# Two-layer attention encoder in float32: where layer B's memory projection runs, how memory turns and grid bias transfers are ordered

## The chip, the cores and the metric

One Trainium2 chip, one of its cores. The metric is device time of one launch in microseconds (us), smaller being better. The core has TensorE (PE, matrix products), VectorE (DVE), ScalarE (ACT), GpSimd (POOL) and SyncE (SP); in this kernel SP issues every transfer, so all transfers stand in one queue in the order in which SP reaches them.

## The reference

The kernel computes two encoder layers over 1024 tokens of width 1024, all in float32. Each layer normalises its input, projects it, runs 12 token heads and 4 memory heads side by side, projects their outputs together, and adds a SwiGLU block of width 2816. Layer A's token heads see a window of 128 tokens either side, with a position bias and a sink logit; layer B's see a neighbourhood on a 16 x 64 grid, with a bias by row and column distance. The memory heads attend to 256 memory rows, normalised with a gain of each layer's own and projected to keys and values:

```python
for i in range(DEPTH):
    h = rms_norm(x, norm_mix_pre[i])
    m = rms_norm(mem, norm_mem[i])
    mkv = jnp.einsum('bmd,de->bme', m, w_mem_kv[i])      # 256 key and 256 value columns
    ...
    mem_out = memory_attn(qm, mk, mv)
    mixed = jnp.einsum('bse,ed->bsd', jnp.concatenate([tok, mem_out], axis=-1), w_out[i])
    x = x + rms_norm(mixed, norm_mix_post[i])
    ...
```

So layer B's memory keys and values depend on the memory alone, and can be made at any time before layer B's memory heads.

## The kernel before, in words

**Arithmetic.** Every product runs as three matmuls (`mm3`, lines 90 to 93) on values split in two: a high part made by ACT (a copy that rounds) and a low part, the remainder, made by DVE or POOL (`split_ps` line 95 from PSUM, `split_raw` line 113 for weights). A weight unit is 128 x 1024 floats: one 512 KB transfer into `wr` (2 buffers), ACT's copy on line 115, the remainder on line 116 (by POOL in the opening, by DVE during the attention: `low`, lines 111 and 609), into a ring of 3 buffers.

**Order.** PE's order is the program's own (the `manual_schedule` blocks of lines 585 and 776). The other engines' instructions and SP's transfers are put in order by a scheduler at build time, by priority (program order, moved by `high_priority` offsets) and by when it estimates them to be ready; an engine then runs its instructions strictly in that order. `keep_in_program_order` ties one instruction behind the one traced just before it on the same engine. `LATER` and `LKS` (60 and 40) lower the priority of the splits of queries and of the opening's keys.

**Opening (lines 585 to 599).** PE turns the 8 normalised token tiles and projects layer A's values from them (`first_values`). Then a loop runs over c = 0, 1. For each c it normalises the two memory tiles with layer c's gain (`memory_rows`), projects the first half of layer A's key unit c (8 steps of 3 matmuls, each 512 columns wide), turns the memory in 4 blocks of 4 transposes (`memory`), projects the second half of the key unit, and runs `memory_kv(c)`: two units by `proj_T` and a pair of units by `proj_N`, 96 matmuls of 256 columns. Layer A's results (c = 0) stay on the chip save one half of the keys; layer B's (c = 1) go to DRAM (`mem_scr`, lines 573 and 574). The projections use two PSUM banks (`psG`), the turns two others (`psT`). Each key half is split into four operand planes by a chain of 4 ACT and 4 DVE instructions on 64 partitions (`k_split`, lines 226 to 229), after which its bank is free. After c = 0 `bias_tables` writes layer A's bias vectors to DRAM (`vec_d`).

**Attention.** `heads` (line 301) walks 8 groups of 16 units in `ORDER` = 0, 6, 1, 7, 2, 3, 4, 5: groups 0 to 5 are pairs of token heads, 6 and 7 pairs of memory heads. A unit is 128 queries of one head. PE does its scores (lines 254 and 255), DVE adds the bias and takes the maximum (269), ACT the exponential (272), POOL the normalisation (274); three units later PE turns the result (282), and two units after that multiplies it with the values (292). Between those, PE is fed with *filler*: the projection that the next group needs, at one step of 3 matmuls per unit, since a group's filler is one query item of 16 steps in layer A (`q_item`). The last group of layer A has no filler:

```python
groups = [(units_by[c], needs[n] if n is not None else []) for c, n in zip(order, order[1:] + [None])]
```

**Queries.** In layer A `q_tiles` (line 203) writes a projected half (512 queries) with one ACT and one DVE instruction on 128 partitions, into `q` and a single-buffered `ql`, and then three SBUF-to-SBUF transfers (`move`, line 201) bring the pieces to their partitions. In layer B it writes them in place, with two ACT and two DVE instructions on 64 partitions (lines 215 to 218) and no transfer. Units 0 to 7 of a group read the first half, units 8 to 15 the second.

**Grid bias.** Layer B's bias table is built in DRAM by 64 small transfers (`grid_tables`, line 367; all issued on line 372): 8 fills from the mask, 32 of `rpb` rows in runs of 32 bytes, 24 from `rpb_d` to `bias_d`. They are traced in five batches of 8, 16, 16, 16 and 8, one when each of pairs 0 to 4 begins, behind that group's bias loads (`bias_tiles`, line 702).

**After the attention** the 8 units of the output projection go through the same ring (lines 853 to 862).

Of the kernel before, what the change touches and what calls it, by code (L numbers as in the profile page):

```python
# [18 lines left out]
P = 128  # L19
D = 1024  # L20
# [46 lines left out]
def build(nc, tc, ctx, x_in, mem_in, wts, t5, onehot, sinks, rpb, maskb, gains, out):  # L67
# [54 lines left out]
    def load_unit(u, where=None, n=3):  # L122
        return split_raw(u, load_raw(u), where or ring, n)

    def proj_T(unit, src, n, dst):

        h, lo = unit
        for c0 in range(0, n, HALF):
# [22 lines left out]
    def run(steps):  # L151
        for _ in steps:
            pass
# [46 lines left out]
    def move(o, i):  # L200
        dma.dma_start(out=o.bitcast(F32), in_=i.bitcast(F32))

    def q_tiles(p, ps, w):

        t = p.tile([P, 2, HALF], F32R, name="q", tag="q", bufs=4)
        if windowed:
            lo = at2.tile([P, HALF], F32R, name="ql", bufs=1)
            nc.scalar.activation(t[:, 0, :w], ps, AF.Copy, scale=SCALE)
            nc.vector.scalar_tensor_tensor(lo[:, :w], ps, SCALE, t[:, 0, :w].bitcast(F32),
                                           ALU.mult, ALU.subtract)  # L210
            move(t[HIGH, 1, :w], t[HIGH, 0, :w])
# [155 lines left out]
    def grid_tables():  # L367

        def go(out, in_):
            return lambda: dma.dma_start(out=out, in_=in_)

        def fill(k, lo, hi, c, m):

            n = (hi - lo) * ROWS
            src = maskb[c * ROWS:(c + 1) * ROWS, m * P:m * P + n]
            return go(rpb_d[k][:, :, lo:hi].rearrange("h r d k -> r h (d k)"),
                      src[:, None].broadcast_to([ROWS, 12, n]))

        fills = [fill(0, lo, min(lo + 8, 31), 0, 0) for lo in range(0, 31, 8)]
        fills += [fill(1, *a) for a in ((0, 7, 7, 1), (7, 15, 0, 0), (15, 23, 0, 0), (23, 31, 0, 3))]
        steps = [fills]
        for k, ds in enumerate((slice(0, 31), slice(7, 23))):
            steps.append([])
            for r in range(ROWS):
                rs = min(max(r - 4, 0), ROWS - 8)
                steps[-1].append(go(rpb_d[k][:, r, ds, rs:rs + 8], rpb[:, ds, 15 - r + rs:23 - r + rs]))
        for k in range(2):
            steps.append([])  # L390
            src = rpb_d[k][0:1, 0:1, 7:8, 0:1]
            for c in range(8):
# [15 lines left out]

    act_d = [dpool.tile([3, FH, P, HALF], F32, name=f"act_d{k}") for k in range(DEPTH)]
    both_d = [dpool.tile([4, FH, P, D], F32, name=f"both_d{k}") for k in range(DEPTH)]  # L410
    mem_scr = dpool.tile([DEPTH, 4, P, 256], F32, name="mem_scr")

    def load_x(t, src, i, grid):
# [77 lines left out]
            return proj_T(unit, src_h, S, put)  # L491
        return (lambda: load_unit(u)), steps, 16 * 1024

    def q_item(u, keep):
        def steps(unit):
            def put(c0, w, ps):
                with tc.high_priority(offset=-LATER):
                    keep(c0 // HALF, q_tiles(a1, ps, w))
            return proj_T(unit, src_h, S, put)
        return (lambda: load_unit(u)), steps, 16 * 1024  # L500

# [14 lines left out]
    def now(item):  # L516
        run(item[1](item[0]()))
# [37 lines left out]
        g = gain(npool, 2 * DEPTH + layer, f"g{layer}")  # L555
        return [norm_rows(npool, raw_tile(mem_in, i), g, 2) for i in range(2)]

    def memory(rows):
        mT = [[a1.tile([P, 2, HALF], F32R, name="mT", tag="q", bufs=4).rearrange(
            "p a (b t) -> p (a b) t", t=MEM) for _ in range(2)] for _ in range(2)]  # L560
        for i in range(2):

            def put(b, pt, i=i):
                split_ps(pt, *(mT[k][b][:, :, i * P:(i + 1) * P] for k in range(2)))

            turn(pp["psT"], "pst", rows[i], put)
        return lambda kc, cs: tuple(mT[k][kc // 4][:, kc % 4, cs] for k in range(2))

    def memory_kv(layer, src):
        def keep(k, ps):  # L570
            if layer or k == 1:
                t = npool.tile([P, 256], F32, name="mraw", bufs=2)
# [7 lines left out]
        u0 = U_MEM + 4 * layer  # L580
        for c in range(2):
# [19 lines left out]
    apart[0] = False  # L601
    grid_todo = grid_tables()

    x_cur = x_in
    for layer in range(DEPTH):
# [61 lines left out]
        def keep_q(c, qts=qts):  # L667
            return lambda half, t: qts.__setitem__((c, half), t)
# [23 lines left out]
        if windowed:  # L692
# [13 lines left out]
            def group(p, order=order):  # L706
                c = p // 3
                pr = pair_of(p, lambda: kts[c], lambda b: vts[b], 2 * c)

                def bias(hh, j):  # L710
                    b = biases[p, hh]
                    if j == 0:
                        return b[:, 1:3]
                    return b[:, 0:2] if j == NT - 1 else b

                def units():
                    if p < 5:
                        bias_tiles(p + 1)
                    for step in grid_todo.pop(0) if grid_todo else []:
                        step()  # L720
                    if p == order[2]:
                        mem_back(1)
                    return units_of(pr, bias, PAIRS_A[p])

                return units, [q_item(U_A + p, keep_q(p))]

            bias_tiles(0)
            um = U_A + 8
        else:
# [6 lines left out]
                    biases[p, hh] = b  # L736

            def kv_items(p):
                its = [k_item(U_B + 6 + p, lambda t: kts.__setitem__(p, t)), q_item(U_B + p, keep_q(p))]
# [29 lines left out]
        for m in range(2):  # L769
            pr = pair_of(6 + m, lambda m=m: mks[m], lambda b: mvs[b], 2 * m)  # L770
            units_by[6 + m] = lambda pr=pr: units_of(pr, None, None)
            needs[6 + m] = [q_item(um + m, keep_q(6 + m))]
        for it in needs[order[0]]:
            now(it)
        groups = [(units_by[c], needs[n] if n is not None else []) for c, n in zip(order, order[1:] + [None])]
        with tc.manual_schedule(engines=PE_ONLY):
            heads(at2, groups)
        low[0] = nc.vector
# [511 lines left out]
```

## Time and profile before

| | us |
|---|---|
| median of 3 runs | 2288.87 (2288.6 to 2290.02) |
| the profiled execution | 2287.94 |
| its span, first to last instruction | 2286.2 |
| PE busy in it | 2152.5 (94%) |
| mean granted TensorE clock | 0.981 of 2.4 GHz |

Times in the rows further down are in us from the span's start. Rows of the timeline are: start, length, engine, line, operation, output<-input, count, and in brackets how long the engine stood idle before and what released it. A matmul's length overlaps its successor's, so how fast PE goes is read from the distance of starts.

### The profile page before, as it was taken

The numbers are of one execution on the slowest core, as the hardware profiler recorded it, in microseconds if no ns is written. First come the engines' busy times: TensorE is split into PE (matmuls) and PEld (weight loads), VectorE is DVE, ScalarE is ACT, GpSimd is POOL, SyncE is SP. The second block draws the span as 40 slices with busy tenths as digits, with TensorE's granted clock in tenths as the row PEclk, the third lists the DMA queues.
The fourth block names the chain that finished last, engine by engine and source line by source line (L and its number), as shares of the span: only waits on it lengthen the run. The fifth ranks groups of instructions, "written<-read, shape, count | busy, mean of one in ns | idle before, by whom it ended". The sixth has DMA issues, their size and how long they took to land. (4 is left out here: it accounts for less than half of the span.)

```text
span 2286.2 us, 31339 instructions
## 1 busy us (share of the span) xinstructions
PE 2152.5 (94%) x10538; PEld 1783.6 (78%) x10538; DVE 1503.4 (66%) x2621; ACT 1062.8 (46%) x2158; POOL 735.5 (32%) x814
## 2 busy tenths in 40 slices
PE   7789987989999999999899999989899999999986
PEld 6678775868888888787788898868688888888865
DVE  5358775578677775556657765765887777755556
ACT  5458885453323332444447765764432333324333
POOL 3336663242333331011115433433334333311012
PEclk9899998999999999999999999999999999999998
DMA  6343344314545453866442322432255555436665
GB/s 218 81 112 89 91 135 105 114 56 159 197 162 182 167 184 108 297 193 211 156 130 70 98 70 77 133 104 104 74 180 184 175 172 180 154 130 223 192 208 168
DMA packets 152600, 333.88 MB, mean 146 GB/s; under 512 B 24791, under 2 KB 47191, under 8 KB 152440
## 3 DMA queue, kind: packets, MB, share of 16 engines
q1 hardware_dynamic: 152440, 331.88, 45.7%
q8 instruction: 84, 1.38, 0.3%
q14 instruction: 76, 0.62, 0.1%
HBM read 226.96 MB, written 92.93 MB: 140 GB/s over the span
## 5 line engine op out<-in xcount | busy, mean ns | idle before, releaser
L944 DVE TENSOR_TENSOR zt<-acc,zt 128x512 f32<-128x512 f32 x300 | 204.6, 686 | 148.8 <-PE acc L93 146.9
L1089 DVE TENSOR_TENSOR dl<-draw,dh 128x1024 fp32r<-128x1024 f32 x146 | 187.0, 1288 | 164.7 <-ACT dh L1087 164.1
L274 POOL TENSOR_TENSOR sn<-sn,st 128x384 f32<-128x384 f32 (+1 forms) x256 | 189.0, 740 | 237.5 <-DVE st L273 199.6
L1087 ACT ACTIVATE dh<-draw 128x1024 fp32r<-128x1024 f32 x146 | 153.9, 1059 | 219.8 <-PE acc L93 141.4
L92 PE MATMUL acc<-dl,dh 128*128 128x512 f32 x584 | 230.6, 395 | 15.8 <-DVE dl L1089 15.8
L93 PE MATMUL acc<-dh,dl 128*128 128x512 f32 x584 | 229.0, 392 | 0.0
L91 PE MATMUL acc<-dh 128*128 128x512 f32 x584 | 225.2, 391 | 1.9 <-ACT dh L1087 1.7
L887 ACT ACTIVATE gh<-zt 128x512 fp32r<-128x512 f32 x168 | 104.3, 628 | 167.2 <-PE acc L92 146.7
L963 POOL TENSOR_TENSOR tw<-tw 128x512 f32<-128x512 f32 x88 | 132.6, 1507 | 120.0 <-DMA tw<-in_wts 114.2
L116 DVE TENSOR_TENSOR wl<-wr,wh 128x1024 fp32r<-128x1024 f32 x88 | 112.8, 1282 | 87.7 <-ACT wh L115 86.0
L1144 POOL TENSOR_TENSOR tt<-tt,g 128x512 f32<-128x512 f32 x32 | 52.9, 1668 | 365.2 <-ACT junk L1143 365.2
L115 ACT ACTIVATE wh<-wr 128x1024 fp32r<-128x1024 f32 x100 | 105.6, 1056 | 119.7 <-DMA wr<-in_wts 85.2
L940 ACT ACTIVATE zt<-zt 128x512 f32<-128x512 f32 x84 | 53.1, 632 | 225.3 <-DVE zt L944 225.3
L963 POOL TENSOR_TENSOR zt<-zt 128x512 f32<-128x512 f32 x66 | 91.4, 1385 | 205.6 <-DVE zt L941 202.2
L92 PE MATMUL psg<-hL,wh 128*128 128x512 f32 x384 | 153.7, 400 | 0.0
L91 PE MATMUL psg<-hH,wh 128*128 128x512 f32 x384 | 153.5, 400 | 0.0
L93 PE MATMUL psg<-hH,wl 128*128 128x512 f32 x384 | 153.4, 399 | 0.0
L292 PE MATMUL psv<-PT,v 128*128 128x256 f32 x656 | 142.2, 317 | 5.2 <-DVE attn L652 3.6
L98 DVE TENSOR_TENSOR PT<-pst,PT 128x384 fp32r<-128x384 f32 (+1 forms) x256 | 126.7, 495 | 28.5 <-ACT PT L97 24.6
L92 PEld LDWEIGHTS acc<-dl,dh 128*128 128x128 f32 x584 | 110.6, 189 | 43.7 <-DVE dl L1089 21.1
L272 ACT ACTIVATE sn<-sn,st 128x385 f32<-128x385 f32 (+3 forms) x192 | 113.0, 589 | 63.7 <-DVE st L269 56.4
L889 DVE TENSOR_TENSOR gl<-zt,gh 128x512 fp32r<-128x512 f32 x168 | 130.1, 776 | 8.1 <-ACT gh L887 8.0
(218 smaller groups left out, 5965.5 us busy)
## 6 DMA issues: line engine op xcount, KB each, us to landing
wr<-in_wts SPq DMA_DIRECT2D x146, 512.0 KB
draw<-both_d SPq DMA_DIRECT2D x88, 512.0 KB
both_d<-zt SPq DMA_DIRECT2D x88, 256.0 KB
tw<-in_wts SPq DMA_DIRECT2D x44, 512.0 KB
both_d<-tw SPq DMA_DIRECT2D x44, 512.0 KB
act_d<-zt SPq DMA_DIRECT2D x66, 256.0 KB
draw<-act_d SPq DMA_DIRECT2D x66, 256.0 KB
draw<-in_wts SPq DMA_DIRECT2D x66, 256.0 KB
```

The costliest lines, as they stand in the source:

```text
L91: nc.tensor.matmul(ps, lh, rh, start=start, stop=False)
L92: nc.tensor.matmul(ps, lh, rl, start=False, stop=False)
L93: nc.tensor.matmul(ps, ll, rh, start=False, stop=stop)
L98: nc.vector.tensor_tensor(ol, ps, oh.bitcast(F32), ALU.subtract)
L272: nc.scalar.activation(sn[:, :m], sn[:, :m], AF.Exp, bias=nm, scale=-1.0, accum_out=ssum)
L274: nc.gpsimd.tensor_tensor(sf, sf, rinv.broadcast_to([P, n]), ALU.mult)
L292: nc.tensor.matmul(pv[:, j % 2], pair.v(self.lo + c)[:, pair.vh + hh], self.PT[:, c], start=c == 0, stop=c == nk - 1)
L889: nc.vector.tensor_tensor(lo, src, h.bitcast(F32), ALU.subtract)
L944: nc.vector.tensor_tensor(o, a, b, ALU.add)
L963: nc.gpsimd.tensor_tensor(o, a, b, ALU.subtract)
L1087: nc.scalar.activation(h, raw, AF.Copy)
L1089: eng.tensor_tensor(lo, raw, h.bitcast(F32), ALU.subtract)
```

## The change

1. `memory` turns a block and then takes two steps of the key projection (`pump`), four times, in place of four turns in a row and then eight steps.
2. For c = 1 the opening only turns the memory; the four turned pieces (high and low, two each, 512 KB a piece) are stored to DRAM (`mt_d`). Layer B's memory projection becomes three filler items (96 matmuls, 4 weight units) of layer A's last group, and pair 4's group begins with loading the four pieces back into a key buffer. The stores of its results to `mem_scr` stay, now from the `sn` buffers that the units use too.
3. In layer A the queries of the first and the last pair (0 and 5) are written in place, as in layer B.
4. Each of the 64 grid bias transfers is tied behind the transfer traced just before it.

`start=0` in `proj_T` is used by nothing here, and the later `apart[0] = False` has no key split of layer A's between its two places.

```diff
-    def q_tiles(p, ps, w):
+    def q_tiles(p, ps, w, apart):
...
-        if windowed:
+        if not apart:
...
         def go(out, in_):
-            return lambda: dma.dma_start(out=out, in_=in_)
+            return lambda: tc.keep_in_program_order(dma.dma_start(out=out, in_=in_))
...
+    mt_d = dpool.tile([2, 2, P, D], F32, name="mt_d")
...
-    def memory(rows):
+    def memory(rows, pump):
...
                 split_ps(pt, *(mT[k][b][:, :, i * P:(i + 1) * P] for k in range(2)))
+                for _ in range(2):
+                    next(pump)
...
-    def memory_kv(layer, src):
+    def memory_items(layer, src, raw_tile):
...
-            run(proj_T(load_unit(u0 + c), src, MEM, lambda c0, w, ps, c=c: keep(c, ps)))
-        run(proj_N([load_unit(u0 + 2), load_unit(u0 + 3)], src, 2, lambda i, ps: keep(2 + i, ps)))
+            its.append((lambda c=c: load_unit(u0 + c),
+                        lambda unit, c=c: proj_T(unit, src(), MEM, lambda c0, w, ps: keep(c, ps)), 8 * 512))
+        its.append((lambda: [load_unit(u0 + 2), load_unit(u0 + 3)],
+                    lambda units: proj_N(units, src(), 2, lambda i, ps: keep(2 + i, ps)), 16 * 512))
+        return its
...
-            src = memory(rows)
+            mT = memory(rows, gen)
+            if c:
+                for k in range(2):
+                    for b in range(2):
+                        dma.dma_start(out=mt_d[k, b], in_=mT[k][b].rearrange("p c t -> p (c t)").bitcast(F32))
             run(gen)
-            memory_kv(c, src)
+            if c == 0:
+                src = mem_src(mT)
+                for it in memory_items(0, lambda: src, lambda: npool.tile([P, 256], F32, name="mraw", bufs=2)):
+                    now(it)
+                bias_tables(npool)
             lk[0] = LK
-            if c == 0:
-                bias_tables(npool)
...
-                return units, [q_item(U_A + p, keep_q(p))]
+                return units, [q_item(U_A + p, keep_q(p), p in (order[0], order[7]))]
...
+        if windowed:
+            back = []
+
+            def reload(then=units_by[order[6]]):
+                t = a1.tile([P, 4, S], F32R, name="mTk", tag="k", bufs=2)
+                for k in range(2):
+                    for b in range(2):
+                        dma.dma_start(out=t[:, 2 * k + b].bitcast(F32), in_=mt_d[k, b])
...
+                return then()
+
+            groups[6] = reload, groups[6][1]
+            groups[7] = groups[7][0], groups[7][1] + memory_items(
+                1, lambda: mem_src(back), lambda: at2.tile([P, 3 * P + 8], F32, name="sn", bufs=TURN + SNX)[:, :256])
```

## Rows read from the trace of the kernel before

**Rows 1.** The page: busy time, share of the span and instructions of each engine.

```profile
PE 2152.5 (94%) x10538; PEld 1783.6 (78%) x10538; DVE 1503.4 (66%) x2621; ACT 1062.8 (46%) x2158; POOL 735.5 (32%) x814
```

**Rows 2.** Busy time by stretch; columns: length, engines (instructions), granted clock, DMA share, GB/s.

```profile
57.00:72.20 15.20, 11.01 (x51) 9.20 (x49) 7.67 (x13) 8.32 (x14) 5.28 (x3) 0.83 0.15 36
98.40:119.60 21.20, 14.54 (x98) 13.61 (x97) 5.70 (x6) 7.82 (x13) 6.21 (x6) 0.84 0.40 120
188.80:216.50 27.70, 27.03 (x166) 23.11 (x165) 23.86 (x77) 25.05 (x70) 20.80 (x41) 1.00 0.33 86
```

**Rows 3.** PE's timeline in the opening: starts that stood idle before.

```profile
53.16 0.66 PE L186 MATMUL pst<-ident,ht 128*128 128x128 f32 x4 [1.12 <-DVE mT L98]
56.26 1.09 PE L186 MATMUL pst<-ident,ht 128*128 128x128 f32 x4 [2.44 <-DVE mT L98]
...
72.18 0.45 PE L91 MATMUL psg<-mT,wh 128*128 128x256 f32 x1 [4.19 <-DVE k L229]
...
91.34 0.93 PE L186 MATMUL pst<-ident,ht 128*128 128x128 f32 x5 [1.12 <-DVE mT L98]
...
137.49 0.55 PE L254 MATMUL pss<-k,q 128*128 128x256 f32 x1 [7.18 <-DMA q<-ql]
```

**Rows 4.** PE's waits, 137.5 to 374: who for whom, total us, times, longest.

```profile
PE pss L254 <- DMA q<-ql: 19.8, 5, 7.2
```

**Rows 5.** PE's timeline in layer A's last pair.

```profile
333.20 0.28 PE L254 MATMUL pss<-k,q 128*128 128x256 f32 x1
...
353.17 0.66 PE L254 MATMUL pss<-k,q 128*128 128x384 f32 x1 [6.36 <-DMA q<-ql]
...
365.58 0.39 PE L254 MATMUL pss<-k,q 128*128 128x256 f32 x1
...
373.84 0.50 PE L91 MATMUL acc<-wh,aoH 128*128 128x512 f32 x1 [1.91 <-ACT aoH L843]
```

**Rows 6.** PE's timeline: starts at full clock, 512 and then 256 columns.

```profile
97.80 0.39 PE L93 MATMUL psg<-hH,wl 128*128 128x512 f32 x1
98.04 0.28 PE L91 MATMUL psg<-mT,wh 128*128 128x256 f32 x1
98.15 0.28 PE L92 MATMUL psg<-mT,wh 128*128 128x256 f32 x1
```

**Rows 7.** Groups by line and shape, 0 to 140: busy us, mean ns, idle before.

```profile
L116 POOL TENSOR_TENSOR wl<-wr,wh 128x1024 fp32r<-128x1024 f32 x12 | 29.7, 2482 | 40.1 <-ACT wh L115 31.0 <-DMA wr<-in_wts 9.1
...
L227 DVE TENSOR_TENSOR k<-psg,k 64x512 fp32r<-64x512 f32 x8 | 5.5, 689 | 19.2 <-ACT k L226 19.1
...
L226 ACT ACTIVATE k<-psg 64x512 fp32r<-64x512 f32 x8 | 4.7, 592 | 7.8 <-PE psg L93 7.3 <-DVE k L229 0.3
```

**Rows 8.** SP's timeline in the opening: the bias vectors' store, the bias loads.

```profile
85.16 0.84 SPq L365 DMA_DIRECT2D vec_d<-both  x1
...
122.19 5.65 SPq L702 DMA_DIRECT2D bias<-vec_d  x8
```

**Rows 9.** Line 372, the grid transfers: SP's ns each, first and last start.

```profile
L372 SPq DMA_DIRECT2D rpb_d<-in_rpb x32: 737/757/1404, 53.6 to 141.9; - x32
L372 SPq DMA_DIRECT2D bias_d<-rpb_d x24: 723/765/791, 142.7 to 305.6; - x24
L372 SPq DMA_DIRECT2D rpb_d<-in_maskb x8: 562/602/714, 23.6 to 52.9; - x8
```

**Rows 10.** SP's timeline when pair 3's group begins.

```profile
272.19 1.74 SPq L702 DMA_DIRECT2D bias<-vec_d  x4
...
274.61 0.55 SPq L201 DMA_DIRECT2D q<-ql  x1
283.61 0.35 SPq L657 DMA_DIRECT2D attn_d<-attn  x1
```

**Rows 11.** DVE's timeline in pair 4: a weight split.

```profile
326.83 1.21 DVE L116 TENSOR_TENSOR wl<-wr,wh 128x1024 fp32r<-128x1024 f32 x1
```

**Rows 12.** POOL's timeline in pair 4: two normalisations twice.

```profile
326.99 2.51 POOL L274 TENSOR_TENSOR sn<-sn,st 128x384 f32<-128x384 f32 x2 [0.16 <-DVE st L273]
...
332.25 1.46 POOL L274 TENSOR_TENSOR sn<-sn,st 128x384 f32<-128x384 f32 x2
```

More of the change, by code (lines that the diff above doesn't have):

```diff
@@ L123, in load_unit, with proj_T @@
         return split_raw(u, load_raw(u), where or ring, n)
-    def proj_T(unit, src, n, dst):
+    def proj_T(unit, src, n, dst, start=0):
         h, lo = unit
-        for c0 in range(0, n, HALF):
+        for c0 in range(start, n, HALF):
             w = min(HALF, n - c0)
@@ L492, in k_item, with q_item @@
         return (lambda: load_unit(u)), steps, 16 * 1024
-    def q_item(u, keep):
+    def q_item(u, keep, apart):
         def steps(unit):
@@ L497, in put @@
                 with tc.high_priority(offset=-LATER):
-                    keep(c0 // HALF, q_tiles(a1, ps, w))
+                    keep(c0 // HALF, q_tiles(a1, ps, w, apart))
             return proj_T(unit, src_h, S, put)
@@ L556, in memory_rows, with mem_src @@
         return [norm_rows(npool, raw_tile(mem_in, i), g, 2) for i in range(2)]
-    def memory(rows):
+    def mem_src(mT):
+        return lambda kc, cs: tuple(t[kc // 4][:, kc % 4, cs] for t in mT)
+    def memory(rows, pump):
         mT = [[a1.tile([P, 2, HALF], F32R, name="mT", tag="q", bufs=4).rearrange(
@@ L564, in put @@
                 split_ps(pt, *(mT[k][b][:, :, i * P:(i + 1) * P] for k in range(2)))
+                for _ in range(2):
+                    next(pump)
             turn(pp["psT"], "pst", rows[i], put)
-        return lambda kc, cs: tuple(mT[k][kc // 4][:, kc % 4, cs] for k in range(2))
-    def memory_kv(layer, src):
+        return mT
+    def memory_items(layer, src, raw_tile):
         def keep(k, ps):
             if layer or k == 1:
-                t = npool.tile([P, 256], F32, name="mraw", bufs=2)
+                t = raw_tile()
                 nc.scalar.activation(t, ps, AF.Copy)
@@ L580, in memory_kv @@
         u0 = U_MEM + 4 * layer
+        its = []
         for c in range(2):
-            run(proj_T(load_unit(u0 + c), src, MEM, lambda c0, w, ps, c=c: keep(c, ps)))
-        run(proj_N([load_unit(u0 + 2), load_unit(u0 + 3)], src, 2, lambda i, ps: keep(2 + i, ps)))
+            its.append((lambda c=c: load_unit(u0 + c),
[3 more added lines that the diff above has]
+        return its
     with tc.manual_schedule(engines=PE_ONLY):
@@ L593, in build @@
                 next(gen)
-            src = memory(rows)
-            run(gen)
-            memory_kv(c, src)
+            mT = memory(rows, gen)
[3 more added lines that the diff above has]
+                        dma.dma_start(out=mt_d[k, b], in_=mT[k][b].rearrange("p c t -> p (c t)").bitcast(F32))
+            run(gen)
+            if c == 0:
[3 more added lines that the diff above has]
+                bias_tables(npool)
             lk[0] = LK
-            if c == 0:
-                bias_tables(npool)
     start.close()
-    apart[0] = False
     grid_todo = grid_tables()
@@ L738, in kv_items @@
             def kv_items(p):
-                its = [k_item(U_B + 6 + p, lambda t: kts.__setitem__(p, t)), q_item(U_B + p, keep_q(p))]
+                its = [k_item(U_B + 6 + p, lambda t: kts.__setitem__(p, t)), q_item(U_B + p, keep_q(p), True)]
                 if p % 2 == 0 and p:
@@ L771, in build @@
             units_by[6 + m] = lambda pr=pr: units_of(pr, None, None)
-            needs[6 + m] = [q_item(um + m, keep_q(6 + m))]
+            needs[6 + m] = [q_item(um + m, keep_q(6 + m), not windowed)]
         for it in needs[order[0]]:
             now(it)
+        apart[0] = False
         groups = [(units_by[c], needs[n] if n is not None else []) for c, n in zip(order, order[1:] + [None])]
+        if windowed:
[5 more added lines that the diff above has]
+                        dma.dma_start(out=t[:, 2 * k + b].bitcast(F32), in_=mt_d[k, b])
+                back.extend([t[:, 2 * k + b].rearrange("p (c t) -> p c t", t=MEM) for b in range(2)]
+                            for k in range(2))
+                return then()
+            groups[6] = reload, groups[6][1]
+            groups[7] = groups[7][0], groups[7][1] + memory_items(
+                1, lambda: mem_src(back), lambda: at2.tile([P, 3 * P + 8], F32, name="sn", bufs=TURN + SNX)[:, :256])
         with tc.manual_schedule(engines=PE_ONLY):
```

## The prediction, made before the changed kernel was run

> **What bounds the kernel now.** I read the page first: PE's matmuls are busy for 94% of the span, DVE for 66% and ACT for 46% [rows 1]. PE's order is written by hand, so what matters is where PE is idle, at its lower clock, or doing work that could stand in an idle place. The change touches only the first 374 us, and I cut these into stretches and looked at PE in each [rows 2]. Three places stand out.
>
> First, the opening. PE waits there for the memory turns (1.12, 2.44 and 1.12 us), for a PSUM bank that the key splits hold (4.19) and for the first queries' transfers (7.18) [rows 3]. The stretch 98.4 to 119.6 holds almost only layer B's memory projection: 21.2 us, of which PE is busy for 14.5, at a granted clock of 0.84 [rows 2], that is at 1.2 GHz for about a third of it; PE had just stood idle.
>
> Second, the second half of a pair's queries. PE's waits for the transfers `q<-ql` come to 19.8 us in five cases [rows 4]: the 7.18 above, 6.36 in the last pair [rows 5], and so 6.2 in the other three (pairs 2, 3 and 4).
>
> Third, the last pair. It runs from 333.20 to 373.84 [rows 5], 40.6 us for 16 units and their drain, while pair 1's group, with filler, takes 27.7 us (188.8 to 216.5) at 98% PE busy and ACT at 90% [rows 2]. So the last pair has room on PE; how little ACT has is seen there too.
>
> **The change part by part.**
>
> *Memory turns between key steps.* For c = 0 the two waits for DVE's split (1.12 + 2.44) [rows 3] are covered: two key steps are 6 matmuls, 1.4 us at the 0.24 us between 512-column starts at full clock [rows 6], and the split that PE waited for has that time and the other PSUM bank's besides. After the waits the clock was low: 0.83 granted over 57.0 to 72.2 [rows 2] means 1.2 GHz for a third of 15.2 us, 5.2 us, in which matmuls took twice as long: 2.6 us lost. So the second key half ends 6.2 us earlier. The 4.19 us wait stays: it is the chain that splits that half, 4 x (0.592 + 0.689) = 5.1 us [rows 7], and it moves as a whole. For c = 1: 1.1 us. Sum **-7.3**.
>
> *Layer B's projection leaves the opening.* The stretch of 21.2 us goes: 96 matmuls, 4 weight loads of 512 KB, 4 ACT copies, 4 splits (POOL's take 2.48 us each [rows 7]), 4 evictions and 4 stores. First queries then follow the key steps directly. Late next is the bank: the second query half needs the bank of c = 1's second key half, freed 5.1 us plus some queueing after that half ends, while the first query half (24 matmuls of 0.24) gives 5.7 us of cover: I add 0.7. Sum **-20.5**.
>
> *First pair's queries in place.* The 7.18 us go: a half is two ACT and two DVE instructions of the shape 64 x 512, 0.592 and 0.689 each on the key splits [rows 7], 2.6 us, and units 0 to 7 need only the half that was projected 5.7 us earlier. Sum **-7.2**.
>
> *What is added in the opening.* Four stores of 512 KB, after the last turn's split. In the new time the opening's turns end near 90 and the first unit would start near 102.5 (137.5 less these three sums, 35.0). The stores hold 2 MB; at the 120 GB/s of the stretch that is cut [rows 2] they would take 17 us, at three times that rate 6. Layer A's bias vectors are stored at 85.16, about 80 in the new time, and the bias loads, issued with the next pair's at 122.19 in 5.65 us [rows 8], must follow all of it in the one queue and land before that. So the cost lies between 0 and about 10 us. I take 0, because the stores start some 12 us before they are in the way; the upper end is a rival. The two query halves take buffers that the stores must have left; these are the first two stored, and have 6 us for it.
>
> *Grid transfers in order.* SP spends 0.60 us on each of 8 fills and 0.76 on each of 56 others, 47 us in all [rows 9]; 40 of the 64 start before 142 [rows 9], in the opening, and cost PE nothing there that I can name. Tied behind the bias loads they come in batches, of which 16 stand behind the loads at 272.19. There the query transfers that follow (one is at 274.61) would go 16 x 0.76 = 12.2 us later; but SP then waits anyway, until 283.61, for an attention tile to be stored [rows 10], 8.4 us. What is left is 3.8. In the other groups the batch fits in such waits or stands in memory pairs' time. Below: the 6.2 us of pairs 2 to 4 could vanish, since the 24 that now run from 142.7 to 305.6, partly in their time, are ordered anew. Above: every issue stands ahead of a query half that PE waits for, +47. I take **+4**, by the row at 272.19, the nearest.
>
> *The last pair.* Its queries in place: -6.4 [rows 5]. Its filler is 96 matmuls of 256 columns, 0.11 us apart, as much PE time as a query item's 48 of 512 at 0.24 [rows 6], about 11 us. So its units should go at a filled pair's pace, 27.7 us for 16 [rows 2]; the drain from the last scores to the output projection was 8.3 us (365.58 to 373.84) [rows 5]. Together 36.0 against 40.6, and less by up to 2 as pair 1 also brings memory keys back: I take **-5**. Its extra work: 4 ACT copies and 4 splits on DVE of 1.21 us [rows 11], where the query item had one each; 4 evictions into `sn` buffers, each held till its store has landed; and the reload of 2 MB, which can start when pair 2 is done, two groups ahead. ACT would come near to full: 25.05 of 27.7 us [rows 2], with one copy and two query instructions in it, and about 3 us more here. The output projection's second and third weights now wait for the last filler's buffers, and have the 8.3 us of the drain for two copies and two splits; its 8 transfers (4 loads, 4 stores) join SP's queue ahead of those weights.
>
> A row bears on these splits: while DVE's split ran from 326.83 to 328.04, POOL's two normalisations took 2.51 us instead of 1.46 [rows 11, 12]. PE lost nothing to it there, as filler covered it, and I price it at nothing. The Trainium skill, SBUF — State Buffer, section "Who interferes with whom", says that a DVE instruction with two SBUF inputs and a GpSimd instruction that reads SBUF exclude each other for the whole instruction; the row agrees (1.05 us). It speaks against moving four such splits from the opening, where POOL made them, to a pair whose units wait for POOL, and is a rival below.
>
> The sum: -7.3 - 20.5 - 7.2 + 0 + 4 - 5 = **-36.0** against the profiled execution's 2287.94 (span 2286.2 and 1.7 around it), so 2251.9. That execution stood 0.9 under the median of the runs, so I say **2253**.
>
> **The rivals.**
>
> *The opening is held by transfers.* Bias loads land 10 us late behind the vectors' store and the 2 MB: 2263. For it: one queue for all; against: 12 us of lead.
>
> *Grid batches ahead of the queries.* Half of the issues count: 47 / 2 in place of 4, 2272. If all do, 2253 - 4 + 47 = 2296, **slower than before**. The place is SP's queue from group 0 to group 6, the price 0.76 us an issue, and it decides from about 40 us (the 36 gained and the 4 already in the sum), that is when more than 53 of the 64 stand ahead of a half that PE needs. For it: the halves' splits have their priority lowered, and three of the six groups wait for them already [rows 4]; against: SP's idle waits take up a part, and the two memory pairs have few transfers of their own.
>
> *Splits and normalisations shut each other out in the last pair.* 4 x 1.05 = 4.2 us if each delay reaches PE: 2257. For it: without filler that pair's turns wait for POOL. Against: pair 4.
>
> *The query waits vanish.* The 6.2 us and the 4 are gained: 2243.
>
> *The tie doesn't bind.* Each transfer is tied only to the one traced before it, a bias load that itself can go a group early; then the batches spread as now and the 4 us fall away: 2249.
>
> **How the numbers follow.** The forecast as summed 0.50; held by transfers 0.15; half the grid issues 0.07, all of them 0.03; shut out 0.07; waits vanish 0.08; tie doesn't bind 0.10. The range 2243 to 2270 takes in all but the grid cases. No change, within 0.2% (4.6 us, about what a measurement here can tell), gets 0.02 from the half case, should it come near its turning point; slower 0.03; faster the rest, 0.95.
>
> **What would show it.** In the changed profile PE's first scores stand near 102.5; no wait of over 1 us at the memory turns; one near 4 us before the second memory unit of c = 0; none for `q<-ql` in pairs 0 and 5. The last pair takes 35 to 36 us, with PE above 85% busy. Line 372 starts after the first scores, and the waits for `q<-ql` in the other pairs come to about 10 us. First scores at 110 or later, or such waits above 25 us, would make me wrong.

## The result and the profile after

The changed kernel takes 2264.69 us (median of 4 runs, 2261.95 to 2271.72), against 2288.73 of the kernel before timed beside it (2288.42 to 2290.02): a ratio of 0.9899 [0.9876, 0.9921]. That is 24.0 us less, inside the range, where 36 had been forecast. The profiled execution took 2261.95, with a span of 2260.2; its profile is called *after* below.

The page's busy times, to be held beside [rows 1]: PE is busy 10.7 us less at the same number of matmuls, so less than half of the 26.0 us that left the span is matmul time; the rest was PE standing idle.

```profile
PE 2141.8 (95%) x10538; PEld 1779.4 (79%) x10538; DVE 1513.8 (67%) x2629; ACT 1064.9 (47%) x2162; POOL 726.2 (32%) x810
```

To find where it went I read the starts on PE's timeline: first scores of the attention, of its last pair, the last scores, and the output projection's first matmul.

| in the span, us | before | after | difference | forecast |
|---|---|---|---|---|
| up to the first scores | 137.49 | 106.77 | -30.7 | -35.0 |
| groups 0 to 6 of the attention | 195.7 | 201.2 | +5.5 | +4 |
| last pair, 16 units | 32.4 | 28.3 | -4.1 | |
| its drain | 8.3 | 11.3 | +3.0 | |
| (last pair with drain) | 40.6 | 39.6 | -1.0 | -5 |
| from the output projection on | 1912.4 | 1912.7 | +0.3 | 0 |

**The opening.** PE's timeline of after, the starts that stood idle before; the third row is the first key step of c = 1, the last the first scores.

```profile
59.59 0.39 PE L91 MATMUL psg<-mT,wh 128*128 128x256 f32 x1 [1.04 <-DVE k L229]
68.02 0.55 PE L91 MATMUL psg<-mT,wh 128*128 128x256 f32 x1 [5.29 <-DVE k L229]
...
80.85 0.50 PE L91 MATMUL psg<-hH,wh 128*128 128x512 f32 x1 [0.40 <-DVE v L98]
...
101.09 0.47 PE L91 MATMUL psg<-hH,wh 128*128 128x512 f32 x1 [1.37 <-DVE k L229]
...
106.77 0.28 PE L254 MATMUL pss<-k,q 128*128 128x256 f32 x1
```

No turn waits any more [rows 3], nor does the first scores' query. But the wait for the key splits, 4.19 before, is now 5.29, and one of 1.04 stands ahead of it. DVE's timeline shows why:

```profile
60.23 0.67 DVE L227 TENSOR_TENSOR k<-psg,k 64x512 fp32r<-64x512 f32 x1
61.05 3.40 DVE L178 SCALAR_TENSOR_TENSOR ht<-xt,r,g 128x1024 f32<-128x1024 f32 x1
64.48 0.68 DVE L229 TENSOR_TENSOR k<-psg,k 64x512 fp32r<-64x512 f32 x1
```

Between two links of the key chain DVE does the normalisation of a memory tile of layer B (line 178), and it takes 3.40 us. The other one of layer B took 1.29 (56.80 to 58.09). POOL's timeline in that place:

```profile
60.98 2.39 POOL L116 TENSOR_TENSOR wl<-wr,wh 128x1024 fp32r<-128x1024 f32 x1
63.83 2.82 POOL L116 TENSOR_TENSOR wl<-wr,wh 128x1024 fp32r<-128x1024 f32 x1 [0.46 <-ACT wh L115]
```

The long one begins 0.07 us behind the first split and ends 1.08 after it. Before the change both normalisations had run (54.23 and 59.94, 1.28 and 1.29 us) ahead of the second half's key chain, the one that PE waits for.

The wait costs more than its length. Busy time by stretch (columns as in [rows 2]; the ninth number is the granted clock), first of after, then of before: from the end of that wait to the first key step of c = 1.

```profile
68.00:80.90 12.90, 12.48 (x75) 11.44 (x75) 2.85 (x6) 4.18 (x7) 2.88 (x5) 0.77 0.25 89
```

```profile
72.10:83.50 11.40, 11.32 (x75) 10.32 (x75) 1.67 (x4) 3.65 (x6) 3.56 (x2) 0.85 0.49 101
```

The same 75 matmuls take 1.5 us longer, at a granted 0.77 in place of 0.85.

**The middle.** PE's waits of after from the first scores to the output projection, against [rows 4]; columns as there.

```profile
PE pss L254 <- DMA q<-ql: 10.2, 2, 6.7
PE pss L254 <- ACT sn L262: 3.9, 4, 2.2
PE pst L282 <- POOL sn L274: 2.5, 3, 1.7
```

The 10.2 us are 6.72 in pair 3's group (at 261.92) and 3.52 in pair 4's (294.17). SP's timeline there answers to [rows 10]:

```profile
241.86 1.74 SPq L717 DMA_DIRECT2D bias<-vec_d  x4
243.65 12.87 SPq L372 DMA_DIRECT2D bias_d<-rpb_d  x16
256.62 0.52 SPq L201 DMA_DIRECT2D q<-q  x1
257.25 0.54 SPq L201 DMA_DIRECT2D q<-ql  x1
257.87 0.54 SPq L672 DMA_DIRECT2D attn_d<-attn  x1
259.15 0.46 SPq L201 DMA_DIRECT2D q<-ql  x1
...
277.31 1.98 SPq L717 DMA_DIRECT2D bias<-vec_d  x4
279.33 6.34 SPq L372 DMA_DIRECT2D bias_d<-rpb_d  x8
285.78 0.77 SPq L201 DMA_DIRECT2D q<-q  x1
```

A batch of 16 stands as one block between the bias loads and the query's moves. Line 372 as a whole (number, ns each, first and last start), against [rows 9]:

```profile
L372 SPq DMA_DIRECT2D rpb_d<-in_rpb x32: 737/757/1855, 138.2 to 211.1; - x32
L372 SPq DMA_DIRECT2D bias_d<-rpb_d x24: 721/724/887, 243.6 to 284.9; - x24
L372 SPq DMA_DIRECT2D rpb_d<-in_maskb x8: 589/602/702, 102.9 to 107.5; - x8
```

The tie binds: only fills start ahead of the first scores (106.77), where 36 of the 64 transfers did before (137.49).

**The last pair.** Busy time of its units and of its drain in after:

```profile
307.90:336.20 28.30, 26.72 (x204) 25.00 (x203) 25.06 (x74) 25.96 (x70) 20.71 (x38) 1.00 0.47 146
336.20:347.60 11.40, 5.59 (x37) 4.40 (x36) 7.74 (x19) 8.82 (x22) 6.13 (x9) 0.82 0.62 172
```

The units go at a filled pair's pace, as forecast; ACT is at 92%. The drain is 3 us longer than in [rows 5]. Its waits on PE, and what DVE and POOL do in it:

```profile
339.39 0.52 PE L282 MATMUL pst<-ident,sn 128*128 128x128 f32 x3 [1.34 <-DVE PT L98]
...
342.86 0.44 PE L282 MATMUL pst<-ident,sn 128*128 128x128 f32 x2 [1.74 <-POOL sn L274]
...
347.52 0.79 PE L91 MATMUL acc<-wh,aoH 128*128 128x512 f32 x1 [2.44 <-ACT aoH L874]
```

```profile
337.17 1.55 DVE L116 TENSOR_TENSOR wl<-wr,wh 128x1024 fp32r<-128x1024 f32 x1 [0.44 <-ACT wh L115]
...
340.42 1.23 DVE L116 TENSOR_TENSOR wl<-wr,wh 128x1024 fp32r<-128x1024 f32 x1
```

```profile
340.52 1.72 POOL L670 TENSOR_TENSOR attn<-pa,pb 64x256 f32<-64x256 f32 x1 [1.04 <-DVE pa L667]
342.20 0.60 POOL L274 TENSOR_TENSOR sn<-sn,st 128x256 f32<-128x256 f32 x1
342.88 0.74 POOL L670 TENSOR_TENSOR attn<-pa,pb 64x256 f32<-64x256 f32 x1
```

Two weight splits of the output projection run on DVE in the drain; in that of before there is none (the first behind the last scores starts at 375.80). The first holds back the split that PE's turn waits for (1.34); beside the second, POOL's addition takes 1.72 in place of 0.74, and PE waits 1.74 for the normalisation queued behind it.

### The profile page after: what moved, and what is told of

Read it like the earlier page. It is cut to its first block, busy times and chain, and to the rows that moved or that the text cites. A ratio compares the mean times of both kernels' runs of the same rounds, so it can differ in the third digit from the quotient of the medians.

```text
span 2260.2 us, 31296 instructions
## 1 busy us (share of the span) xinstructions
PE 2141.8 (95%) x10538; PEld 1779.4 (79%) x10538; DVE 1513.8 (67%) x2629; ACT 1064.9 (47%) x2162; POOL 726.2 (32%) x810
## 5 line engine op out<-in xcount | busy, mean ns | idle before, releaser
L1175 POOL TENSOR_TENSOR tt<-tt,g 128x512 f32<-128x512 f32 x32 | 52.2, 1643 | 363.9 <-ACT junk L1174 310.8
L116 DVE TENSOR_TENSOR wl<-wr,wh 128x1024 fp32r<-128x1024 f32 x92 | 118.2, 1285 | 67.3 <-ACT wh L115 65.5
```

The costliest lines, as they stand in the source:

```text
L116: b = low[0].tensor_tensor(lo, raw, h.bitcast(F32), ALU.subtract)
```

## The experiments

Twelve runs, in three sets of four with the kernel before timed beside each set; kernels of different sets are compared by their ratio to it. All start from the changed kernel. The table gives medians, and from each kernel's one profile the first scores, three lengths and the output projection's start, in us.

| kernel | median us | ratio | first scores | pair 3 | pair 4 | last pair + drain | out. proj. |
|---|---|---|---|---|---|---|---|
| changed, again | 2263.94 | 0.9891 [0.9874, 0.9909] | 106.0 | 37.1 | 32.1 | 29.4 + 11.6 | 350.7 |
| grid_free | 2256.5 | 0.986 [0.9843, 0.9877] | 106.0 | 27.2 | 32.9 | 29.1 + 11.6 | 339.0 |
| turns_in_a_row | 2270.03 | 0.9919 [0.9903, 0.9935] | 110.6 | 36.7 | 30.3 | 28.4 + 11.4 | 352.6 |
| proj_in_opening | 2280.08 | 0.9965 [0.9952, 0.9977] | 125.3 | 36.0 | 31.8 | 25.9 + 8.3 | 363.9 |
| q05_moves | 2272.99 | 0.9924 [0.9903, 0.9945] | 115.1 | 37.4 | 31.9 | 27.5 + 13.4 | 357.0 |
| norm_late | 2263.09 | 0.9883 [0.9862, 0.9903] | 103.0 | 36.7 | 31.8 | 28.5 + 11.9 | 346.3 |
| q34_in_place | 2265.74 | 0.989 [0.9869, 0.9912] | 106.5 | 28.2 | 28.2 | 35.4 + 16.5 | 349.5 |
| fill_early | 2268.02 | 0.9904 [0.9876, 0.9932] | 105.8 | 37.1 | 31.7 | 35.4 + 8.4 | 353.0 |
| tie_first_40 | 2264.43 | 0.9892 [0.9875, 0.991] | 106.0 | 31.6 | 33.8 | 28.0 + 11.9 | 345.9 |
| free_late | 2255.37 | 0.9853 [0.9833, 0.9872] | 104.1 | 27.5 | 32.8 | 28.7 + 11.2 | 337.2 |
| free_late_split | 2260.65 | 0.9872 [0.9854, 0.989] | 103.4 | 27.4 | 41.5 | 23.7 + 13.6 | 342.6 |
| free_late_q4 | 2256.38 | 0.9859 [0.9843, 0.9875] | 103.5 | 27.9 | 27.8 | 36.3 + 11.7 | 340.2 |

**The changed kernel again** was the yardstick for the next three, with no edit.

> The changed kernel once more, unaltered, to see how far its times spread and in which stage. If the stages are fixed by the instruction order, the first scores start at 106 to 108 us, the output projection at 346 to 349, and what differs between executions lies behind 374 us of the kernel before. If the spread of about 10 us between its executions comes from the moved part, the start of the output projection moves by several us while the rest stays at 1912 to 1913.

The time came out as before: 2263.94 (2263.61 to 2264.83). The stages did not quite: first scores at 106.0, but pair 3's group, pair 4's and the last pair's units each took 1.1 to 1.3 us longer than in the first profile (35.8, 30.8 and 28.3), so that the output projection began at 350.7, behind the 346 to 349 expected; the rest took 1911.6. So a difference of a us or so in one group, between two profiles, need not come from an edit.

**No tie.**

```diff
-            return lambda: tc.keep_in_program_order(dma.dma_start(out=out, in_=in_))
+            return lambda: dma.dma_start(out=out, in_=in_)
```

> The changed kernel without the tie on the 64 grid transfers. Theory: the tie costs the two query waits at 262 and 294 us (6.7 and 3.5) and gives nothing back on PE in the opening, so without it pair 3's group falls from 35.8 to about 31 us and the time by 4 to 5 us. Rival: in the opening the untied transfers stand ahead of the weight loads, the four memory stores and the bias loads, so the first scores start 3 to 10 us later than 106.8 and the time does not fall or rises.

The time falls by 7.4 us, more than the 4 to 5 expected, and the first scores stay at 106.0. So the tie loses time, and no transfer of the grid bias holds the opening in either form. Pair 3's group falls by 9.9. SP's timeline there, and the busy time of the group in the changed kernel (again) and in this one:

```profile
238.87 1.73 SPq L717 DMA_DIRECT2D bias<-vec_d  x4
240.70 0.50 SPq L201 DMA_DIRECT2D q<-q  x1
241.29 0.54 SPq L201 DMA_DIRECT2D q<-ql  x1
```

```profile
240.50:277.60 37.10, 29.84 (x170) 25.85 (x169) 24.48 (x77) 24.75 (x68) 20.44 (x42) 0.86 0.55 159
```

```profile
238.30:265.50 27.20, 27.18 (x171) 23.35 (x170) 22.32 (x75) 23.90 (x67) 20.64 (x42) 1.00 0.53 152
```

The moves follow the bias loads at once, and the wait of 6.9 us goes. The other 2.7 us are PE's own: its matmuls are busy for 27.18 us in place of 29.84, since the clock stays at 1.00 where it was granted 0.86 over the group with the wait. That is the stretch right behind the wait (it ends at 261.27), at the lower of the two clock levels:

```profile
261.30:266.00 4.70, 4.70 (x15) 4.20 (x16) 2.30 (x6) 1.95 (x5) 0.95 (x2) 0.50 1.02 305
```

**Turns in a row.** The turns as before the change, all else as changed.

```diff
-                for _ in range(2):
-                    next(pump)
```

> The changed kernel with the four memory turns in a row and the eight key steps behind them. By the sum (7.3 us for the interleaving) the first scores start at about 114 us instead of 106.8. By what the changed profile shows (the second memory unit of c = 0 started 4.2 us earlier and the low clock lasted longer behind it, 2.6 us at the next keys; 1.1 for c = 1) the interleaving is worth 3 to 4: first scores at 110 to 111.

First scores 4.6 us later, time 6.1 us longer. PE's timeline has the waits of [rows 3] again, 1.12, 2.44 and 1.12 us at the turns, and 4.19 ahead of the second memory unit, at 70.58.

**The projection in the opening.** Layer B's memory projection back where it was.

```diff
-            if c == 0:
-                src = mem_src(mT)
-                for it in memory_items(0, lambda: src, lambda: npool.tile([P, 256], F32, name="mraw", bufs=2)):
-                    now(it)
+            src = mem_src(mT)
+            for it in memory_items(c, lambda: src, lambda: npool.tile([P, 256], F32, name="mraw", bufs=2)):
+                now(it)
...
-            groups[7] = groups[7][0], groups[7][1] + memory_items(
```

> The changed kernel with layer B's memory projection back in the opening, and so without the four stores, the reload and the last pair's filler; turns, queries in place and tie stay. By the sum, the first scores start 20 us later, near 127. The last pair, with its query wait gone and no filler, should then show what the filler and its splits cost there: if the 39.6 us it takes now are the filler's, it falls to about 33 (27.7 less the wait of 6.4 is not reachable, but 40.6 - 6.4 = 34 is); if it is bound by its own chain, it stays at 37 to 39. Time: 2264.7 + 20 - 6 = 2279 by the first, 2284 by the second.

First scores 19.3 us later, time 16.1 us longer. Part of that is a wait that the changed kernel doesn't have: 6.14 us for the first memory pair's queries (at 155.78), by which pair 0's group takes 30.4 us in place of 26.1. The run also shows the last pair with its queries in place and no filler: 25.9 us of units and 8.3 of drain, 34.2 in all. The filler, some 11 us of matmuls, adds 5.4 to 6.8 us to that (39.6 and 41.0 in the two profiles of the changed kernel). So about half of it is hidden; the forecast, 36.0 against 34.2, had left 1.8 us for the rest.

**Moves in pairs 0 and 5.**

```diff
-                return units, [q_item(U_A + p, keep_q(p), p in (order[0], order[7]))]
+                return units, [q_item(U_A + p, keep_q(p), False)]
```

> The changed kernel with the queries of the first and the last pair brought by transfers again. By the sum, 7.2 us at the first scores (106 to about 113) and 6.4 in the last pair, 2278 in all. Rivals: in the opening the transfers now also queue behind 2 MB of stores and the bias loads, so first scores come at 116 or later; in the last pair the filler and its four weight splits keep PE busy while the transfers run, so that the pair's units take 28 to 31 us and the wait is 0 to 3.

PE's first scores come at 115.1, behind the only long wait for a query in pair 0:

```profile
115.14 0.55 PE L254 MATMUL pss<-k,q 128*128 128x256 f32 x1 [8.97 <-DMA q<-ql]
```

That is 9.1 us for the first pair, more than the 7.18 before. In the last pair no wait for `q<-ql` appears, and it takes 40.9 us with its drain, against 41.0: with filler in it, writing its queries in place is worth nothing that shows here.

**The normalisation late.** ACT's squares of layer B's memory tiles are kept in their traced place, so that DVE's normalisation comes behind the key chain.

```diff
-        nc.scalar.activation(ht, xt, AF.Square, scale=ROOT, accum_out=ss)
+        a = nc.scalar.activation(ht, xt, AF.Square, scale=ROOT, accum_out=ss)
+        if pin:
+            tc.keep_in_program_order(a)
```

> The changed kernel with c = 1's two memory normalisations held back, on ACT, until c = 0's projections are evicted. Theory: the 3.40 us normalisation on DVE (1.28 elsewhere) next to POOL's weight split is what lengthens PE's wait for the second memory unit from 4.2 to 5.3; without it that wait falls to 3 or less, the unit starts near 65.5 us in place of 68.0, and the first scores at 103 to 104 in place of 106 to 107. Rival: the wait is the key split's own chain of 5.1 us and stays at 4 to 5; first scores at 105 to 106.

DVE and PE at the place in question:

```profile
78.37 1.28 DVE L180 SCALAR_TENSOR_TENSOR ht<-xt,r,g 128x1024 f32<-128x1024 f32 x1 [0.66 <-POOL r L165]
81.30 1.28 DVE L180 SCALAR_TENSOR_TENSOR ht<-xt,r,g 128x1024 f32<-128x1024 f32 x1 [0.45 <-POOL r L165]
```

```profile
65.52 0.55 PE L91 MATMUL psg<-mT,wh 128*128 128x256 f32 x1 [4.14 <-DVE k L231]
```

Both normalisations take 1.28 us, the wait of 1.04 is gone, the other is back to 4.14 and ends 2.5 us earlier, and the first scores come at 103.0, near the forecast's 102.5. The length of the wait is as the rival said (4 to 5, the chain's own), the first scores as the theory did. From the first DVE link of the second half's chain to the last it is 4.73 us here (59.94 to 64.67), against 6.95 in after (60.23 to 67.18): 2.2 us, near the 2.1 by which the normalisation between them was longer. So most of the opening's shortfall was this instruction. The run takes it out of the chain and away from POOL's split at once, so it doesn't part the two. The time itself is 0.9883 [0.9862, 0.9903], not told apart from the changed kernel's.

**Queries of pairs 3 and 4 in place.**

```diff
-                return units, [q_item(U_A + p, keep_q(p), p in (order[0], order[7]))]
+                return units, [q_item(U_A + p, keep_q(p), p in (0, 3, 4, 5))]
```

> The changed kernel with the queries of pairs 3 and 4 written in place as well. Theory: the waits of 6.7 to 6.9 and 3.3 to 3.5 us at their second halves are the 16 and 8 grid issues of 0.76 us ahead of their transfers in SP's queue; in place, both waits go, pair 3's group falls from 36 to about 28 us and pair 4's from 31 to 28, and the time by 10 us, to 2254. Rival: ACT and DVE, 90% busy in a filled group, take the two more instructions a half badly, and half of it comes back as longer units: 2259.

Both waits go and the two groups fall to 28.2 us each, 12.8 us together. The last pair gives back 10.9 of them, at 51.9 us with its drain against 41.0. PE's waits there:

```profile
PE acc L91 <- ACT aoH L874: 4.7, 1, 4.7
PE pst L282 <- DVE PT L98: 4.2, 2, 3.8
PE psg L91 <- ACT wh L115: 3.0, 1, 3.0
```

PE now waits for a weight of the filler, which SP began to load at 309.87 only; in the changed kernel SP issued loads at 292.30 and 309.70, with 307.9 the start of the last pair there and 297.6 here.

**The filler paced faster**, so that the last pair's weights leave the ring sooner:

```diff
-                    while done < cost * (2 * n + part + 1) / (2 * len(units)):
+                    while done < cost * min(1, (2 * n + part + 1) / (2 * len(units)) * (1.25 if len(its) == 3 and windowed else 1)):
```

> The changed kernel with the last pair's filler handed out a quarter faster, so that it ends at unit 13 of 16. Theory: the drain grew from 8.3 to 11.3 us because the splits of the output projection's second and third weights wait for the filler's weight buffers, fall into the drain and hold POOL up there; with the buffers free three units earlier, the drain falls to 9 us or less, and the units take up to 1.5 us more: 1 to 2 us faster. Rival: the drain is long because the last results' stores hold buffers that the units use, or the filler itself is too much; then the drain stays above 10 and the units grow as well, and the time does not fall.

The drain is back at 8.4 us, as before the change, and no weight split runs on DVE in it (one starts at 342.41, ahead of the last scores at 344.63, the next at 354.99, behind the output projection's start). That bears out that the splits were its 3 us. But the units take 35.4 us in place of 29.4, where 1.5 more had been expected, and the time is 0.9904 [0.9876, 0.9932]: it was moved, not saved.

**The tie on the first 40 only**, the last 24 (`rpb_d` to `bias_d`) free.

```diff
-                        step()
+                        step(p < 3)
```

> Only the 8 fills and the 32 rpb transfers of the grid bias keep their tie; the 24 from rpb_d to bias_d (the batches of pairs 3 and 4) are free as before the change. Theory (the tie costs through the two waits for q<-ql that stand behind those two batches, 6.9 and 3.3 us in the changed kernel): pair 3's group, 37 us, falls to 27 to 29, at most one wait for q<-ql is left in pairs 3 and 4, of under 4 us, and the ratio to the kernel before comes to about 0.986 to 0.987, as without any tie. Rival (the rpb batches cost as much, in the groups of the first memory pair and pair 1, which are 2 and 1 us longer than before the change): half of the 7.5 us comes back, ratio about 0.9875. Second rival (the freed 24 stay where they are, since the tied ones ahead of them set their place): nothing changes, 0.989.

Pair 3's group falls to 31.6 us and its wait to 1.76, but pair 4's wait grows to 4.74 and the time stays at 0.9892 [0.9875, 0.991]. The theory is wrong: both waits are left, and no time is gained. SP's timeline in pair 4's group:

```profile
272.88 1.73 SPq L717 DMA_DIRECT2D bias<-vec_d  x4
274.65 5.39 SPq L372 DMA_DIRECT2D bias_d<-rpb_d  x7
280.08 0.56 SPq L105 DMA_DIRECT2D wr<-in_wts  x1
280.75 0.51 SPq L201 DMA_DIRECT2D q<-q  x1
```

Sixteen of the 24 copy the table that the first 16 rpb transfers fill (all issued by 155.4), and five of them go from 160.06 on; the last eight copy the other table, which is written until 212.7. So 4 in place of 16 are left ahead of pair 3's moves (243.52 to 246.58), but 7 stand ahead of pair 4's, and there the second rival holds. The first rival holds in part too: the groups of the first memory pair and of pair 1 stay at 27.5 and 28.7 us, against 25.3 and 27.9 without any tie. Of the 11.7 us that the kernel without any tie gained up to the output projection, this one gains 4.9; its median shows none of that, and why the rest of the run gives it back wasn't found.

**No tie, and the normalisation late**, the two edits above together.

> No grid transfer is tied, and ACT's squares of layer B's memory normalisation are kept in their traced place, so that this normalisation stands behind the key splits of c = 0. Theory (the two act on different waits): first scores near 103, as in the kernel with the late normalisation alone, group lengths as in the kernel without ties, time about 2253 to 2255, ratio 0.984 to 0.985. Rival (what the earlier start gains is given back in pair 4 and the last pair, as the late normalisation alone gained 1 us of its 3): the time stays at that of the kernel without ties, ratio 0.986.

2255.37 us, 0.9853 [0.9833, 0.9872]: the lowest median of the study, with the output projection at 337.2. The intervals of this and of the kernel without the tie overlap, so the late normalisation isn't shown to add anything. That the tie's removal gains is shown by its own set: its slowest run took 2259.42, the fastest of the changed kernel 2263.61.

**The filler split over two groups**, on top of that: the two key units in pair 4's group.

```diff
+            groups[6] = reload, groups[6][1] + its[:2]
+            groups[7] = groups[7][0], groups[7][1] + its[2:]
```

> As the kernel with free grid transfers and late normalisation, but the two key units of layer B's memory projection (two fillers of 24 matmuls) run in pair 4's group behind the last pair's queries, and only the pair of value units (48 matmuls) in the last pair. Theory (the last pair's filler costs because four weight units queue ahead of the output projection's, whose splits then fall in the drain, 11.5 us instead of 8.3): pair 4's group grows by at most the 5.3 us of those 48 matmuls, less what its idle time takes (about 3 us of waits there), so by 2 to 4; the last pair falls from 29 to 26 to 27 and the drain to 8 to 9.5: 2 to 4 us less in all. Rival (PE has no room in pair 4's group and the last pair stays held by its own turns): pair 4's group grows by 5, the last pair falls by under 5, and the time is the same or up to 3 us longer.

The rival holds, and falls short: the last pair's units fall by 5.0 us to 23.7, but pair 4's group grows by 8.7, in place of 5, and the drain by 2.4:

```profile
263.80:305.30 41.50, 34.70 (x219) 31.07 (x218) 30.72 (x85) 30.70 (x78) 21.24 (x42) 0.96 0.65 205
```

PE is busy 34.7 us there, against 29.0 of 32.8 in the kernel above: their 48 matmuls come on top, and 3.10 us more are a new wait for a bank that a query's split holds.

**Pair 4's queries in place too**, on the kernel without tie and with the late normalisation.

```diff
-                return units, [q_item(U_A + p, keep_q(p), p in (order[0], order[7]))]
+                return units, [q_item(U_A + p, keep_q(p), p in (0, 4, 5))]
```

> As the kernel with free grid transfers and late normalisation, with pair 4's queries written in place too, in pair 3's group. Theory (the one wait for q<-ql left without ties, 3.7 us in pair 4's group, goes): pair 4's group 33 falls to 29 to 30, ratio about 0.0015 lower. Rival (as when the queries of pairs 3 and 4 were written in place, weight loads of the last pair come late once pair 4's group is shorter): the last pair and its drain, 40.7 us, grow by as much, and the time stays.

The rival holds again: pair 4's group falls by 5.0 us, and the last pair's units grow by 7.6. The chain is seen on ACT and PE:

```profile
294.76 0.59 ACT L218 ACTIVATE q<-psg 64x512 fp32r<-64x512 f32 x1
295.37 2.01 ACT L115 ACTIVATE wh<-wr 128x1024 fp32r<-128x1024 f32 x2
```

```profile
296.48 0.58 PE L91 MATMUL psg<-mTk,wh 128*128 128x256 f32 x1 [3.90 <-ACT wh L115]
```

The filler's first weight was loaded from 276.61 on, but in ACT's order its copy stands behind the last query half of the group before. A shorter group before brings the filler's first step nearer to that copy.

## Why the prediction was right, and where it fell short

Faster, and the range, held. Of the 36.0 us forecast in the profiled execution 26.0 came. By its steps:

- **Memory turns, -7.3: the step that was off in the opening.** The waits at the turns went, and the granted clock over 53 to 68 us was 0.97, against 0.77 before. The second key half ended at 58.55 in place of 65.12, 6.6 us earlier where 6.2 had been forecast; the clock's share of that, 2.6 by the granted clock, is 2.4 by PE's rows of before (twelve starts from 57.00 to 62.17, 0.43 apart in place of 0.23). But "it moves as a whole" was wrong of the 4.19 us wait: 1.04 + 1.10 were added, the second memory unit began at 68.02 in place of 66.0, and 1.5 us more were lost to the lower clock behind it. The key steps of c = 1 came 2.6 us earlier, not 6.2. The run with the turns in a row prices the step at 4.6. With the normalisations late the unit began at 65.52, so the chain does move as a whole where nothing comes between its links. What came between is a rival that I had put in the last pair: a DVE instruction and a POOL weight split shutting each other out. It bit in the opening, on the normalisation, which went from 1.29 to 3.40 us. The Trainium skill, SBUF — State Buffer, section "Who interferes with whom", says that a DVE instruction with two SBUF inputs and a GpSimd instruction that reads SBUF exclude each other. The two rows agree (3.40 us beside POOL's split of 2.39), and so does the run that moved the normalisation (1.28).
- **Projection out of the opening, -20.5; first queries, -7.2.** From the first key step of c = 1 to the first scores it was 54.0 us and is 25.9; with the 1.1 at the turn the forecast had 28.8 less, and 28.1 it is. The bank wait is 1.37, where I added 0.7. Undone one at a time, the projection is worth 19.3 and the queries 9.1.
- **Added stores, 0.** Right: SP had issued the four by 96.53 and the bias loads by 102.84, and nothing of PE's waits for them before 106.77.
- **Grid transfers, +4.** Right against the kernel before (+5.5, with the groups of the first memory pair and of pair 1 longer by 1.9 and 1.0, pair 3's by 4.4, and pair 2's wait of 2.1 gone), and the mechanism was the one named: 16 issues of 12.87 us ahead of pair 3's moves. The fills began at 102.9, not behind the first scores, and cost them nothing (106.0 with the tie and without). As the price of the tie it was too small, for I took the waits of before as what there would be without it. The kernel without the tie has one wait of 3.7 us left, and is 7.4 us faster. So the rival that the query waits vanish was true in part of the rest of the change, and the tie hid it: without the tie groups 0 to 6 take 192.3 us, 3.4 less than before, where the rival had 6.2. The clock's share wasn't in my sum either: 2.7 of the 9.9 us in pair 3's group.
- **Last pair, -5: the other step that failed, -1.0.** The units are right (28.3 against 27.7). The drain was taken at 8.3 and is 11.3: I had named the output projection's splits, "two copies and two splits" in the drain, and priced them at nothing. The run with the faster filler brings it back to 8.4 with no such split in it, which bears out the cause, though it is no gain. PE was busy for 81% of the pair with its drain, not above 85%. And -6.4 for the queries and the filler's hidden time were counted on the same idle place: with its drain the pair takes 40.6 us with the moves alone, 40.9 with moves and filler, 34.2 with neither, and 39.6 to 41.0 with the filler alone.

Open stay two things: why the time from the output projection's start on varies among these kernels (1909.8 to 1915.9 us, one profile each), which have the same code there, and whether another place for the filler's weights in ACT's and SP's order would let the gains of the last two groups stand.

## What to carry to other kernels

A wait and filler compete for the same idle time: price them together, on the stretch without either. When a chain of groups shares one ring of weights, a group made shorter shows its gain only if the next group's weights, their copies and their splits move up too; look at where the static order of the other engines has put them. And price a forced order against what the free order would give after the change, not against the waits seen before it.

## What the runs showed of the hardware

A wait of PE can cost more than its own length: behind one of 6.9 us the granted clock was 0.50 for 4.7 us, and the group's matmuls took 2.7 us longer in all. And instructions on DVE and POOL that have nothing to wait for from each other in the program can still hold each other up: 3.40 us for one of 1.28 on DVE beside a weight split on POOL, 1.72 for one of 0.74 on POOL beside a split on DVE.
